# A two-layer hybrid attention trunk: TensorE's order written by hand as phases of the attention, instead of an order that a scheduler finds for whole blocks

## The chip, the cores and the metric

The kernel runs as one launch on one core of a Trainium2 chip. The metric is the device time of that launch in microseconds (us), the median over runs. The core has engines that run side by side and wait for one another by semaphores: TensorE (PE; its weight loads are listed as PEld), VectorE (DVE), ScalarE (ACT), GpSimd (POOL), and SyncE (SP), whose queue issues the transfers from DRAM.

## What is computed

One sequence of 256 tokens with 1024 features passes two layers. Eight heads of 64 columns ("MoBA") attend causally with a distance bias; eight more ("NSA", two groups of keys) sum three gated branches: compressed keys, selected blocks and a window. At 256 tokens every selection takes all that is causal, so the selected and the window branch are plain causal attentions over two sets of keys. The core of the reference:

```python
cs = silu(c)
for l in range(2):
    mod = cs @ w_ada[l] + b_ada[l]                       # 3072 columns
    shift, scale, gate = split(mod, 3)
    h = rmsnorm(x, g_pre[l]) * (1 + scale) + shift
    u = h @ w_in[l]                                      # 1024 x 3864
    qm, km, vm, zm, qn, kc, vc, ks, vs, kw, vw, gl, zn = split(u)
    o_m = softmax(causal(qm km' / 8 - slope * distance)) @ vm
    kc, vc = compress(kc), compress(vc)                  # 32-token windows, stride 16, two matmuls and a gelu
    o_n = g0 * attend(qn, kc, vc) + g1 * attend(qn, ks, vs) + g2 * attend(qn, kw, vw)
    y = concat(o_m * silu(zm), o_n * silu(zn))
    x = x + gate * rmsnorm(y @ w_out[l], g_post[l])
```

## The kernel before

**Projections.** Each projection is carried in two float32r parts of both operands: VectorE or ScalarE rounds a float32 tile to its high part, and VectorE subtracts to get the low part. `mm3` then issues three matmuls per row block of 128 features (low x high, high x low, high x high, L399 to L401). Weights come in units of 512 KB: a transfer into a `raw` tile (a pool of 8), the high part (`hi`, L364 on ScalarE or L366 on VectorE), the low part (`lo`, L372, VectorE). A chunk of 256 columns of `w_in` is two units and 48 matmuls. A chunk that is read with the weights stationary (`col_chunk`) does its columns in two halves of 24 matmuls.

**Modulation.** The sums of `silu(c) @ w_ada` are made in groups of 512 columns, four units of 512 KB each: either on VectorE, with 1 + 7 multiply-adds of 128x512 into `acc` (L231, L233) and four matmuls against ones (L240), or on TensorE with 32 small matmuls per group (L216). Then ScalarE copies the sums (`accr`, L245) and TensorE transposes them into columns (L252), so that VectorE can add the bias (L259).

**Attention.** An NSA block is two heads. Per head and token tile there are two score matmuls (L586, L587) into an `sc` bank of PSUM, and a softmax: VectorE adds the bias and takes the row's extreme (L545), ScalarE takes the exponential with its sum (L548), VectorE the reciprocal (L550) and the gate, and one of the two scales the row (L555, L557), all in an `S` tile (a pool of 3). Then three transposes on TensorE per branch (L565) and a copy to `PT` (L570, a pool of 3), and the value matmuls (L596, L602, L604) into the one `av` bank, of which head 0 writes the upper and head 1 the lower 64 partitions. The matmuls of the branches follow head after head. A MoBA block is the same with one branch (scores L615, L617, values L627, L630). `gate_out` (L637 to L641) multiplies by the gate path `z` and splits the result into `yH` and `yL`.

**The output.** `out_mm(0)` is 96 matmuls for the first 128 tokens, `out_mm(1)` 96 for the second. `post` squares the result on ScalarE (L309), takes the power -0.5 on POOL (L305), multiplies by the gate rows (L689) and updates `x` (L692). `hnorm` then squares `x` again, takes the power, scales (L322), transposes on TensorE (L336) and writes the next layer's `hH`, `hL` (L344 to L347).

**What sets the order.** Only the first layer's start (`first_layer_start`: the first modulation, the norm, and the first 2,000 or so columns) is issued in written order on all engines. What follows is a list of step names, `PLAN`. Each step emits whole blocks ("0nsa0", "0km0", "0out0"), and a tile scheduler moves the instructions of all engines, TensorE's too, as far as their dependencies and its own priorities let it; a choice of engine may be attached to a step (`:p` puts a modulation sum on TensorE, `:d` rounds the high parts on VectorE). The order about the layer boundary is "0out0 0post0 1h0 0out1 0post1 1V00 1h1 1V10".

## Time and profile before

| | us |
|---|---|
| median of three runs (lowest, highest) | 356.02 (354.57, 357.14) |
| span of the profiled execution, first to last instruction | 354.4 |
| TensorE busy | 341.4 |
| VectorE busy | 266.1 |
| ScalarE busy | 204.3 |
| POOL busy | 10.5 |

The profile is of one execution. Its span is 1.6 us under the median of the runs, within their spread; what lies before the first and after the last instruction is not in it, and no other time of this execution is listed. A busy TensorE is not the same as one at its best: matmuls overlap, and one that is listed with 0.28 us can follow the last by 0.12 us, so distances from start to start are what counts there. In the rows, "L399" is a line of the kernel, `pj<-hH,lo` says that a tile `pj` is written from `hH` and `lo`, and "xN" that N instructions are put together.

### The profile page before, as it was taken

The page shows a single profiled execution, that of the slowest core. Times are in us where ns is not written, and L with a number is a line of the kernel's source. Part 1 is how long each engine was busy: PE and PEld are TensorE (multiplying, and loading weights), DVE is VectorE, ACT ScalarE, POOL GpSimd, SP SyncE. Part 2 cuts the span into 40 slices and gives each one's busy share as a digit, 9 for nine tenths or more (in the row PEclk, how much of TensorE's full clock was granted, in tenths as well). Part 3 has the DMA queues.
Part 4 walks back from the last instruction along what each step waited for, and adds up shares of the span by engine and source line. Part 5 has one row for each costly group of instructions (what it writes and reads, how often), then busy time and mean ns, then how long its engine had stood idle before and what let it go on. Part 6 is the DMA issues. An engine that isn't in the chain of part 4 may idle for free.

```text
span 354.4 us, 7595 instructions
## 1 busy us (share of the span) xinstructions
PE 341.4 (96%) x2852; PEld 299.6 (85%) x2852; DVE 266.1 (75%) x727; ACT 204.3 (58%) x506; POOL 10.5 (3%) x23
## 2 busy tenths in 40 slices
PE   7999999999999999989999999999999999999993
PEld 7789889988887878767998999998878898677993
DVE  2648669999987898879898985999987646776132
ACT  4423407776989863757365455543889655668211
POOL 2000001100000000000011000000000000000000
PEclk9999999999999999999999999999999999999998
DMA  7999999939955566899755798489454330000111
GB/s 237 321 331 353 350 338 220 308 108 354 347 186 154 167 217 210 259 351 333 197 149 162 223 284 247 130 285 352 130 160 139 119 120 2 0 2 1 62 60 59
DMA packets 72060, 71.12 MB, mean 201 GB/s; under 512 B 11440, under 2 KB 61784, under 8 KB 72024
## 3 DMA queue, kind: packets, MB, share of 16 engines
q1 hardware_dynamic: 72024, 70.65, 64.1%
q8 instruction: 22, 0.36, 0.4%
q14 instruction: 14, 0.11, 0.1%
HBM read 69.58 MB, written 1.06 MB: 199 GB/s over the span
## 4 chain that ended last, share of the span: by engine, by line
PE 73%; DVE 13%; DMA 6%; issue 4%; ACT 2%; POOL 1%; SPq 1%; DVEq 0%; POOLq 0%; ACTq 0%
PE pj L399 13%; PE pj L400 13%; PE pj L401 13%; PE tr L565 5%; DVE lo L372 4%; PE av L602 3%; PE tr L216 3%; DMA yL<-in_w_ada_dram 2%; DMA raw<-in_w_out_dram 2%; PE av L627 2%; PE sc L586 2%; PE sc L617 2%; PE av L604 2%; PE pj L839 2%; PE av L596 2%
## 5 line engine op out<-in xcount | busy, mean ns | idle before, releaser
L372 DVE TENSOR_TENSOR lo<-raw,hi 128x1024 fp32r<-128x1024 f32 (+3 forms) x82 | 90.7, 1123 | 15.9 <-ACT hi L364 15.5
L399 PE MATMUL pj<-hH,lo 128*128 128x256 f32 x320 | 93.1, 291 | 0.0
L400 PE MATMUL pj<-hL,hi 128*128 128x256 f32 x320 | 92.5, 289 | 0.0
L401 PE MATMUL pj<-hH,hi 128*128 128x256 f32 x320 | 92.1, 288 | 0.0
L364 ACT CAST hi<-raw 128x1024 fp32r<-128x1024 f32 (+4 forms) x70 | 66.0, 966 | 22.7 <-PE pj L401 17.1
L399 PEld LDWEIGHTS pj<-hH,lo 128*128 128x128 f32 x320 | 61.0, 191 | 4.4 <-issue 3.4
L400 PEld LDWEIGHTS pj<-hL,hi 128*128 128x128 f32 x320 | 61.0, 191 | 2.2 <-issue 1.7
L401 PEld LDWEIGHTS pj<-hH,hi 128*128 128x128 f32 x320 | 61.0, 191 | 1.4 <-issue 1.1
L548 ACT ACTIVATE S<-S,mn 128x128 f32<-128x128 f32 (+1 forms) x96 | 42.7, 448 | 4.4 <-DVE mn L545 4.1
L233 DVE SCALAR_TENSOR_TENSOR acc<-raw,cs,acc 128x512 f32<-128x512 f32 x49 | 36.5, 747 | 1.6 <-DMA raw<-in_w_ada_dram 1.2
L545 DVE CUSTOM_DVE_ANT_0 S<-sc,bias 128x128 f32<-128x128 f32 (+1 forms) x96 | 31.6, 350 | 7.6 <-PE tr L565 3.1
L399 PE MATMUL pj<-hi,yL 128*128 128x256 f32 x112 | 31.9, 285 | 0.0
L401 PE MATMUL pj<-hi,yH 128*128 128x256 f32 x112 | 31.9, 286 | 0.0
L400 PE MATMUL pj<-lo,yH 128*128 128x256 f32 x112 | 31.8, 285 | 0.0
L565 PE MATMUL tr<-ident,S 128*128 128x128 f32 x144 | 29.6, 281 | 0.0
L570 ACT COPY PT<-tr 128x384 f32<-128x384 f32 x44 | 20.3, 478 | 10.0 <-PE tr L565 9.9
L565 PEld LDWEIGHTS tr<-ident,S 128*128 128x128 f32 x144 | 17.5, 140 | 6.7 <-issue 3.0
L555 ACT ACTIVATE S<-S,sm 128x256 f32<-128x256 f32 (+1 forms) x46 | 20.4, 483 | 2.9 <-DVE sm L550 1.4
L399 PEld LDWEIGHTS pj<-hi,yL 128*128 128x128 f32 x112 | 21.2, 189 | 0.9 <-issue 0.9
L401 PEld LDWEIGHTS pj<-hi,yH 128*128 128x128 f32 x112 | 21.1, 189 | 0.5 <-issue 0.5
L400 PEld LDWEIGHTS pj<-lo,yH 128*128 128x128 f32 x112 | 21.0, 188 | 0.3 <-issue 0.3
L548 ACT ACTIVATION_READ_ACCUMULATOR S<-S,mn 128x1 f32 x96 | 18.3, 190 | 0.0
(248 smaller groups left out, 650.1 us busy)
## 6 DMA issues: line engine op xcount, KB each, us to landing
raw<-in_w_in_dram SPq DMA_DIRECT2D x43, 512.0 KB, 4.5
raw<-in_w_ada_dram SPq DMA_DIRECT2D x32, 512.0 KB, 4.6
raw<-in_w_out_dram SPq DMA_DIRECT2D x16, 512.0 KB, 7.2
raw<-in_w_in_dram SPq DMA_DIRECT2D x9, 256.0 KB, 3.9
qs<-in_w_ada_dram SPq DMA_DIRECT2D x4, 512.0 KB, 7.2
yH<-in_w_ada_dram SPq DMA_DIRECT2D x4, 512.0 KB, 7.2
yL<-in_w_ada_dram SPq DMA_DIRECT2D x4, 512.0 KB
raw<-in_w_in_dram SPq DMA_DIRECT2D x9, 128.0 KB, 5.7
```

What stands on the lines that cost most here:

```text
L216: self.nc.tensor.matmul(pm[32 * r:32 * r + 32, :P], self.csz[:, k, :], raw[:, j, c * P:(c + 1) * P], start=first <= k < first + turns, sto ...
L233: nc.vector.scalar_tensor_tensor(out=out, in0=raw[:, j], scalar=self.cs[:, k:k + 1], in1=out, op0=OP.mult, op1=OP.add)
L364: self.nc.scalar.copy(hi[:, :nk * n], raw[:, :nk * n])
L372: self.nc.vector.tensor_sub(lo[:, :nk * n], raw[:, :nk * n], hi[:, :nk * n].bitcast(F32))
L399: nc.tensor.matmul(out, aL, bH, start=first, stop=False)
L400: nc.tensor.matmul(out, aH, bL, start=False, stop=False)
L401: nc.tensor.matmul(out, aH, bH, start=False, stop=last)
L545: nc.vector.tensor_tensor_reduce(out=s[:, a:b], in0=sc[:, a:b], in1=self.bias[:, h, S - (b - a):S], scale=-1.0, scalar=3.0e38, op0=OP.add, ...
L548: nc.scalar.activation(s[:, a:b], s[:, a:b], AF.Exp, bias=mn[:, i:i + 1], scale=-1.0, accum_out=sm[:, i:i + 1])
L555: nc.scalar.activation(s[:, a:b], s[:, a:b], AF.Copy, scale=sm[:, i:i + 1])
L565: nc.tensor.transpose(pt[:, i * P:(i + 1) * P], blk, self.ident)
L570: nc.scalar.copy(ps, pt[:, :3 * P])
```

## The change

After the first layer's start, TensorE's instructions are issued in the written order; the other engines are still ordered by the scheduler. The steps are cut smaller. `nSbj` is the scores and softmax of NSA block b, head j; `nTbj` its six transposes in a row; `nVb` the block's values, with the two heads alternating. `mSb`, `mTb`, `mVb` are the same of a MoBA block, both heads together. `c0` to `c4` are the five pieces of the compressed branch. Names with a point are pieces of projections of 24 matmuls ("zn1.0"; the out pieces have 12 or 24). `g0`, `g1`, `x1` to `x4` are the ends of modulation groups; their weights are fetched and summed on VectorE (`ada_start`) from the place of the group before. Weights of a projection are fetched and split four pieces ahead of the first use (`AHEAD`). The plan:

```python
PLANS = ["""
c0 nS00 zn1.0 nS01 c1 g0 zn1.1 nT00 c2 nS10 vm.0 nT01 c3 vm.1 nS11 km0.0 c4 nT10 nS20 km0.1 nV0 g1
nT11 qm0.0 nS21 nV1 G qm0.1 nT20 nS30 zm0.0 nT21 nS31 zm0.1 nV2 x0 x1 km1.0 nT30 mS0 km1.1 nT31 x2
qm1.0 nV3 mT0 mS1 qm1.1 mV0 x3 zm1.0 mT1 mS2 zm1.1 mV1 x4 out0.0 out0.1 mT2 mS3 out1.0 mV2 out1.1
mT3 out1.2 mV3 out0.2 out0.3 post0
out1.3 out1.4 out1.5 post1
""", """
h0 A.0 V0.0 V1.0 h1 A.1 V0.1 V1.1 K.0 K.1 Q0.0 Q0.1 nS00 C.0 nS01 C.1 nT00 Q1.0 c0 nT01 Q1.1 c1
nS10 zn0.0 c2 nS11 zn0.1 c3 qm0.0 nT10 c4 qm0.1 nV0 nS20 km0.0 nT11 nS21 km0.1 nV1 g0 nT20 zn1.0
...
```

The core of the diff:

```diff
-        pm = self.tl(self.ps, [P, 512], "tr", bufs=2)
-        if on_pe:
-            for i, raw in enumerate(units):
-                self.ada_on_pe(pm, spec, i, raw)
-        else:
-            self.ada_sum(pm, self.ada_on_dve(spec, units))
-        self.ada_cols(spec, self.ada_rows(pm))
+    def ada_end(self, spec):
+        acc = self.acc.pop(spec[0])
+        pc = self.tl(self.ps, [P, 512], "tr", bufs=2)
+        for j in range(4):
+            self.nc.tensor.matmul(pc[:, j:j + 1], acc[:, j * P:(j + 1) * P], self.ones[:, 0:1],
+                                  start=True, stop=True)
+        self.ada_mod(spec, pc[:, :4])
...
-        for i in range(2):
-            for j in range(2):
-                o = av[j * HD:(j + 1) * HD, :]
-                vc = slice(i * P + g * HD, i * P + (g + 1) * HD)
-                nc.tensor.matmul(o[:, :S], self.vsw[:, 0, vc], pts[j][i][:, :S],
-                                 start=False, stop=False)
-                nc.tensor.matmul(o[:, P:S], self.vsw[:, 1, vc], pts[j][i][:, S:],
-                                 start=False, stop=(i == 1))
+        for kt in range(2):
+            for i in range(2):
+                vc = slice(i * P + g * HD, i * P + (g + 1) * HD)
+                for j in range(2):
+                    if kt == 0:
+                        nc.tensor.matmul(o[j][:, :S], self.vsw[:, 0, vc], pts[j][i][:, :S],
+                                         start=False, stop=False)
+                    else:
+                        nc.tensor.matmul(o[j][:, P:S], self.vsw[:, 1, vc], pts[j][i][:, S:],
+                                         start=False, stop=(i == 1))
...
+            if c == "out0":
+                c = "out0" if int(t.split(".")[1]) < (2, 3)[int(t[3])] else "out1"
+            if (l, c) not in seen:
+                seen.add((l, c))
+                loads.setdefault(pieces[max(0, at - AHEAD)], []).append((l, c))
+        adas = [i for i, (_, t) in enumerate(steps) if t[0] in "gx" and t != "x0"]
+        for at, i in enumerate(adas):
+            before = adas[at - 1] + 1 if at else 0
+            loads.setdefault(before, []).append(steps[i])
...
-            self.rp = self.pool("raw", bufs=8)
+            self.rp = self.pool("raw", bufs=5)
...
-            self.wp = self.pool("work", bufs=3)
-            self.pp = self.pool("probT", bufs=3)
+            self.wp = self.pool("work", bufs=6)
+            self.pp = self.pool("probT", bufs=6)
...
             with self.tc.manual_schedule():
                 started = self.first_layer_start()
-            self.first_layer_rest(*started)
-            for token in PLAN:
-                self.step(token)
+            with self.tc.manual_schedule(engines={mybir.EngineType.PE}):
+                self.first_layer_rest(*started)
+                self.after_start()
```

`work` holds the `S` tiles of the softmax. The choices of engine by step are gone: transposed probabilities are always copied by ScalarE, and the high parts of weights are rounded on VectorE in two chunks only (`1V0`, `1V1`). In layer 0 all modulation groups are now summed on VectorE.

The first place at which the order changes is TensorE's, right after the first layer's start. `pj_936` and `pj_1071` are the chunk "zn1", L469 and now L482 the first matmul of the compressed branch (with `cmpR` and its weights `raw`), L605 and L606 NSA scores. TensorE before:

```order
L437 MATMUL tr_895<-ident,pe_892 128x32
L399 MATMUL pj_936<-hH_167,lo_928 128x256
L400 MATMUL pj_936<-hL_168,hi_926 128x256
L401 MATMUL pj_936<-hH_167,hi_926 128x256
...
L469 MATMUL sc_995<-cmpR_897,raw_987 64x33
L469 MATMUL sc_995<-cmpR_897,raw_989 64x33
```

And TensorE with the change:

```order
L450 MATMUL tr_897<-ident,pe_894 128x32
L482 MATMUL sc_951<-cmpR_899,raw_943 64x33
L482 MATMUL sc_951<-cmpR_899,raw_945 64x33
...
L605 MATMUL sc_1001<-wide_885,qs_135_911 128x256
L606 MATMUL sc_1001<-wide_884,qs_135_911 128x256
...
L418 MATMUL pj_1071<-hH_167,hi_1031 128x256
```

The 48 matmuls of "zn1", which stood ahead of the compressed branch, are now behind it and behind the first scores.

The transfers moved with it. In SyncE's queue of before the weights of "zn1" (`raw_924`, `raw_930`) go out during the first layer's start; now they stand behind a modulation group and the compressed branch's weights, which take six places of a pool of five. SyncE with the change, where `raw_1029` and `raw_1035` are "zn1":

```order
L212 DMA raw_932<-in_w_ada_dram 128x2x512
L473 DMA raw_943<-in_w_ck_dram 128x16x64
L473 DMA raw_945<-in_w_cv_dram 128x16x64
L478 DMA w_145_947<-in_w_cv_dram 64x64
...
L447 DMA pe_3111<-in_pe_v_dram 16x128
L373 DMA raw_1029<-in_w_in_dram 128x4x256
L373 DMA raw_1035<-in_w_in_dram 128x4x256
L373 DMA raw_1041<-in_w_in_dram 128x3x280
```

The program makes `raw_1029` and `raw_1035` wait for TensorE's last reads of `raw_943` and `raw_945`, which are the L482 matmuls above.

The second place is VectorE's order at the layer boundary. `x_97` and `x_99` are the two token tiles of the residual, `pj_2494` and `sc_2376`/`sc_2401` pieces of `out1`, `wide_2462` and `wide_2601` the scaled `x` that `h0` transposes. VectorE before:

```order
L692 SCALAR_TENSOR_TENSOR x_97<-wide_2444,rstd_2452,x_97 128x512
...
L303 SCALAR_TENSOR_TENSOR rstd_2466<-ssq_2463 128x1
L372 TENSOR_TENSOR lo_2617<-raw_2613,hi_2615 128x1024
L322 TENSOR_SCALAR wide_2462<-x_97,rstd_2466 128x512 x2
...
L689 TENSOR_TENSOR wide_2593<-pj_2494,modG_1868 128x512
```

VectorE with the change:

```order
L730 SCALAR_TENSOR_TENSOR x_97<-wide_2492,rstd_2500,x_97 128x512 x2
...
L727 TENSOR_TENSOR wide_2578<-sc_2401,modG_1598 128x256
L730 SCALAR_TENSOR_TENSOR x_99<-wide_2578,rstd_2591,x_99 128x512 x2
L320 SCALAR_TENSOR_TENSOR rstd_2605<-ssq_2602 128x1
L389 TENSOR_TENSOR lo_2700<-raw_2695,hi_2698 128x1024
L339 TENSOR_SCALAR wide_2601<-x_97,rstd_2605 128x512 x2
```

`h0`'s norm (`rstd_2466`, now `rstd_2605`) stood ahead of `post1`; now the whole of `post1`, up to the update of `x_99`, stands ahead of it.

The third is TensorE's order at the same boundary (L336, now L353, are `h0`'s transposes). Before, the transposes lie among the matmuls of `out1`:

```order
L336 MATMUL tr_2472<-ident,wide_2462 128x128 x4
L336 MATMUL tr_2483<-ident,wide_2462 128x128 x4
...
L401 MATMUL pj_2495<-hi_1734,yH_1148 128x256
...
L401 MATMUL sc_2496<-hi_2314,yH_1148 128x256
...
L401 MATMUL pj_2625<-hi_2615,hH_2458 128x256
```

With the change they follow the last of `out1`, and the next layer's chunk "A" follows them at once:

```order
L418 MATMUL sc_2376<-hi_2269,yH_999 128x256
...
L418 MATMUL sc_2401<-hi_2275,yH_999 128x256
L353 MATMUL tr_2611<-ident,wide_2601 128x128 x4
L353 MATMUL tr_2622<-ident,wide_2601 128x128 x4
...
L418 MATMUL pj_2633<-qm_2450,hH_2597 128x280
```

Between `out0`'s last matmul and `h0`'s transposes there are now 48 matmuls of `out1` (`out1.3` to `out1.5`); the other 48 come before `out0.2`.

## Rows read from the trace of the kernel before

**Rows 1.** The page's chain that ended last: shares of the span by engine.

```profile
PE 73%; DVE 13%; DMA 6%; issue 4%; ACT 2%; POOL 1%; SPq 1%; DVEq 0%; POOLq 0%; ACTq 0%
```

**Rows 2.** Waits of TensorE, longest sums: us in total, times, longest.

```profile
PE tr L252 <- ACT accr L245: 2.0, 3, 1.2
PE tr L336 <- DVE wide L322: 1.2, 2, 0.7
PE pj L400 <- DVE lo L372: 0.9, 1, 0.9
```

**Rows 3.** Stretches of the span: length, busy us by engine, granted clock, DMA share, GB/s.

```profile
75.50:174.70 99.20, 97.86 (x791) 81.27 (x792) 86.12 (x274) 69.52 (x191) 0.00 (x0) 1.00 0.79 253
240.00:348.50 108.50, 108.34 (x815) 91.31 (x813) 69.03 (x241) 64.89 (x183) 0.55 (x1) 1.00 0.28 91
348.50:351.00 2.50, 0.03 (x1) 0.00 (x0) 1.48 (x4) 0.47 (x2) 0.55 (x1) 1.00 0.00 0
351.00:354.40 3.40, 0.00 (x0) 0.00 (x0) 0.43 (x1) 0.00 (x0) 0.00 (x0) 0.51 0.40 154
```

**Rows 4.** VectorE's groups by line and shape: count, busy us, mean ns.

```profile
L372 DVE TENSOR_TENSOR lo<-raw,hi 128x1024 fp32r<-128x1024 f32 x67 | 81.0, 1218 | 15.9 <-ACT hi L364 15.5
L233 DVE SCALAR_TENSOR_TENSOR acc<-raw,cs,acc 128x512 f32<-128x512 f32 x49 | 36.5, 747 | 1.6 <-DMA raw<-in_w_ada_dram 1.2
```

**Rows 5.** Timeline of TensorE at an NSA block: start us, us, instructions.

```profile
101.68 0.66 PE L602 MATMUL av<-PT,vsw 128*64 128x256 f32 x4
102.16 0.40 PE L604 MATMUL av<-PT,vsw 128*64 128x128 f32 x4
102.38 0.59 PE L602 MATMUL av<-PT,vsw 128*64 128x256 f32 x2
102.81 0.38 PE L604 MATMUL av<-PT,vsw 128*64 128x128 f32 x2
103.12 0.44 PE L565 MATMUL tr<-ident,S 128*128 128x128 f32 x2
...
104.47 0.28 PE L401 MATMUL pj<-hH,hi 128*128 128x256 f32 x1
104.68 0.65 PE L596 MATMUL av<-pct,vx 128*64 128x256 f32 x4
105.26 0.39 PE L399 MATMUL pj<-hH,lo 128*128 128x256 f32 x1
105.48 0.28 PE L400 MATMUL pj<-hL,hi 128*128 128x256 f32 x1
```

**Rows 6.** Timeline after the first layer's start, TensorE and VectorE.

```profile
66.25 0.25 PE L437 MATMUL tr<-ident,pe 32*128 32x32 f32 x1
...
70.88 0.19 DVE L450 COPY cmpR<-tr 128x16 f32<-128x16 f32 x1
...
72.37 2.06 PE L469 MATMUL sc<-cmpR,raw 128*64 128x33 f32 x64
...
73.94 0.69 DVE L753 SCALAR_TENSOR_TENSOR z<-z,tr 128x512 f32<-128x512 f32 x1
```

**Rows 7.** The page's DMA issues of 512 KB: KB, median us to landing.

```profile
raw<-in_w_in_dram SPq DMA_DIRECT2D x43, 512.0 KB, 4.5
```

**Rows 8.** Timeline of the layer boundary: VectorE, POOL, TensorE.

```profile
174.68 0.69 DVE L689 TENSOR_TENSOR wide<-pj,modG 128x512 f32<-128x512 f32 x1 [0.22 <-ACT S L309]
...
180.24 1.47 POOL L305 TENSOR_TENSOR rstd<-rstd,half 128x1 f32<-128x1 f32 x1 [2.95 <-DVE rstd L303]
181.74 0.88 DVE L322 TENSOR_SCALAR wide<-x,rstd 128x512 f32<-128x512 f32 x2 [0.45 <-POOL rstd L305]
182.37 1.07 PE L336 MATMUL tr<-ident,wide 128*128 128x128 f32 x8 [0.55 <-DVE wide L322]
```

**Rows 9.** The first stretches of TensorE, its warming matmuls of 128 columns (L283) alone.

```profile
2.50:6.30 3.80, 3.73 (x17) 3.74 (x18) 1.00 0.93 338
6.30:7.30 1.00, 1.00 (x11) 1.00 (x9) 1.00 0.98 280
```

More of the change, by code (lines that the diff above doesn't have):

```diff
@@ new lines, in piece @@
+    def piece(self, l, c, i):
+        if c[:3] == "out":
+            return self.out_piece(int(c[3]), i)
+        n = int(c[-1]) if c[-1].isdigit() else 0
+        w = self.w[c]
+        if c == "vm":
+            self.tok_mm(i, w, self.ev_v(self.VM0, 512))
+        elif c == "A":
+            self.tok_mm(i, w, self.ev_a)
+        elif c[0] == "V":
+            if self.first("vm", l):
+                self.vm = self.tl(self.mp, [P, NT, 512], "vm")
+            self.tok_mm(i, w, self.ev_v(256 * n, 256 * n + 256))
+        elif c[:2] in ("zn", "zm"):
+            side = c[1] == "n"
+            if self.first(c[:2], l):
+                self.z[side] = self.tl(self.mp, [P, 4, S], f"z{side:d}")
+            self.col_piece(w, i, self.ev_z(side, n))
+        elif c[:2] in ("qm", "km"):
@@ new lines, in step @@
+            {"nS": self.nsa_scores, "nT": self.nsa_turn, "nV": self.nsa_values,
+             "mS": self.moba_scores, "mT": self.moba_turn, "mV": self.moba_values}[kind](*n)
+        elif kind == "g":
+            self.ada_end(self.spec(token))
+        elif kind == "x" and n[0] == 0:
+            self.mod_rows()
+        elif kind == "x":
+            self.ada_end(self.spec(token))
+        elif kind == "G":
+            self.G = self.gate_rows()
+        elif kind == "post":
+            self.post(l, n[0], self.pos(n[0]), self.G)
+        elif kind == "h":
+            if n[0] == 0:
+                self.start_layer()
+            self.hnorm(n[0])
@@ new lines, in spec, with plan @@
+    def spec(self, token):
+        i = int(token[1:])
+        return [(2, 4 * i, 4)] if token[0] == "g" else [((i - 1) // 2, 4 * ((i - 1) % 2), 4)]
+    def plan(self):
+        steps = [(l, t) for l, p in enumerate(PLANS) for t in p.split()]
+        pieces = [i for i, (_, t) in enumerate(steps) if "." in t]
+        loads = {}
+        seen = set()
+        for at, i in enumerate(pieces):
+            l, t = steps[i]
+            c = t.split(".")[0]
+            if c == "out1":
+                c = "out0"
+            if c == "out0":
[7 more added lines that the diff above has]
+            loads.setdefault(before, []).append(steps[i])
+        rows = [i for i, (_, t) in enumerate(steps) if t == "x0"][0]
+        loads.setdefault(rows - 20, []).append((0, "rows"))
+        return steps, loads
@@ new lines, in after_start @@
+    def after_start(self):
+        steps, loads = self.plan()
+        for i, (l, t) in enumerate(steps):
+            for ll, c in loads.get(i, ()):
+                if c == "rows":
+                    self.load_mod_rows(1)
+                elif c[0] in "gx":
+                    self.ada_start(ll + (c[0] == "x"), self.spec(c))
+                else:
+                    self.load_chunk(ll, c)
+            if "." in t:
+                c, p = t.split(".")
+                self.piece(l, c, int(p))
+            else:
+                self.step(l, t)
```

304 lines of the change are left out of this document (137 added, 167 removed).

## The prediction

> **What bounds the kernel now.** I read the chain first, then TensorE's waits, then stretches of the span, then single places. The chain is 73% TensorE and 13% VectorE [rows 1]. TensorE's listed waits come to about 6 us in all, and the largest sum is 2.0 us [rows 2], so over the whole span it is the bound, and what can be won on it must come from the length of its own work. The stretches tell more [rows 3]. Between 75.5 and 174.7 us, the attention and the projections of layer 0, TensorE is busy 97.9 of 99.2 us, but VectorE is busy 86.1 as well: there it is a second bound close behind. Between 240 and 348.5, the same part of layer 1, TensorE is busy 108.3 of 108.5 us and VectorE only 69.0. So a gain on TensorE counts in full in layer 1, and in layer 0 only as far as VectorE lets it. The reader is to keep these two halves apart.
>
> **The change part by part.**
>
> *TensorE's own work.* A break between float32r projections and a float32 piece costs time on both sides. At 104.47 the last projection matmul is followed after 0.21 us, and at 105.26 the first one after a break is followed by the next after 0.22 us [rows 5]; in a run of one kind 256 columns take 0.12 (four L602 in 0.48, same rows). So a break costs about 0.09 + 0.10 = 0.19 us. Counted in the two orders from the end of the first layer's start, TensorE leaves the projections 120 times before and 45 times with the change: 75 x 0.19 = 14.3 us. Alternating heads: four matmuls of 256 and four of 128 columns with alternating heads take 0.70 us (101.68 to 102.38), two and two of one head 0.74 (102.38 to 103.12) [rows 5]. Two and two alternated would be 0.35, so a group of four gains 0.39. The values of both layers are 192 such passes, 48 groups, at most 18.7 us; in the block shown only a third was not alternated already, so 6; the MoBA scores, which now alternate too, I put at 2. Together with some sums and transposes of the modulation that go (at most 2 us, within the range), I take 24 us off TensorE, 13 in layer 0 and 11 in layer 1; the bounds are 14 (breaks alone) and 35.
>
> *VectorE's work in layer 0.* Between the evacuation of the first gate path (73.94 [rows 6]) and `post0`'s first multiplication (174.68 [rows 8]) VectorE's two orders differ so: 13 more multiply-adds of 128x512, one more first product, 5 more low parts of 1024 columns, two of 840 and one of 560, one rounding to high parts; the rest nearly cancels. They come from the modulation groups that were summed on TensorE or later, and from low parts that are now made before the boundary. At 0.747 and 1.218 us [rows 4]: 13 x 0.75 = 9.8, 5 x 1.22 = 6.1, by width 2 x 1.0 and 0.7, and at most 0.75 and 1.2 for the other two: 20.5. Neighbours overlap a little, so I use 18, with 16 and 20.5 as bounds. The stretch was busy 86.1 us plus the 1.6 before its start, 87.7 of 100.7. With 18 more it is 105.7: the multiplication can't come before 73.9 + 105.7 = 179.6, even if VectorE never waits. It waited 13.0 us before. With twice the softmax buffers and weights fetched four pieces ahead I take a third of that, 4 us: 183.6, or +8.9; bounds +3 (16, no wait) and +20 (18, the old wait). So the 13 us that TensorE saves here are not seen at all.
>
> *The start of that stretch.* TensorE comes free at 66.25; VectorE ends `cmpR` at 70.88 + 0.19 = 71.07; the compressed branch's matmuls take 2.1 us [rows 6]. Before, the 48 matmuls of "zn1" covered the wait. Now nothing does, and "zn1" has no weights until those matmuls release its two buffers: issued at 73.2, 4.5 us to landing [rows 7], a rounding and a low part of at most 1.2 each: 80.1. TensorE idles 4.8 + 6.2 = 11.0 us less the 0.7 of the first scores, about 10. That costs nothing beyond the above: TensorE would have 174.7 - 13 + 10 = 171.7, plus 5.8 for the 48 matmuls of `out1` that now go ahead of `out0`'s end, 177.5, which is still under VectorE's 179.6. It only takes away the slack. If the transfer lands in 2 us, the wait is 7.5, and nothing changes.
>
> *The layer boundary.* P is `post0`'s first multiplication. Before, `h0`'s transposes start 7.7 us after it (182.37 [rows 8]), and TensorE has 96 matmuls of `out1`, 11.5 us, to cover that; the two waits for the scaled `x` are 1.2 us together [rows 2]. Now 48 are left, 5.8 us, and end at about P + 7 (`out0` ends 1 us after P). On VectorE `h0`'s norm is queued behind all of `post1`: a square (0.6), a power on POOL (up to 1.47 [rows 8]; I take 1.0), two updates of `x` at 0.75, then the norm's own square, power (1.47) and the first scaling (0.5): P + 12.5. TensorE idles 5.5. "A" then follows the transposes at once, and must wait for all of `hH` and `hL` of that token tile: I estimate 4 us (twelve pieces of 0.3 to 0.7 us on two engines, with a POOL power of the second tile queued in front of `hL`), and 2 more at "A.1" behind `h1`. In all 11.5 us idle in the place of 1.2, less the 5.8 that were done earlier: +4.5. Bounds 0 (VectorE, freer by now, makes the pieces at once) and +8.
>
> *Layer 1.* TensorE saves 11. New waits: the first scores stand directly behind the queries' chunk (2 us); `c4` has one piece of 24 matmuls and six transposes as cover, 3.5 us, for a chain on VectorE in which six multiply-adds and one low part are mixed, 6 x 0.75 + 1.2 + 2.5 = 8.2: 4.7 us; transposes that wait for one of two banks, 2. About 9, bounds 2 and 12. Net -2. VectorE has room [rows 3]. The tail after TensorE's end, 348.5 to 354.4, is unchanged.
>
> **The sum.** +8.9 +4.5 -2 = +11.4 us on the profiled span of 354.4: 365.8. The median of the runs stands 1.6 above it, so 367; I say 366, since the waits in layer 0 are the softest term.
>
> **The rivals.**
>
> *The waits are hidden and layer 1 wins (faster).* If VectorE never idles in layer 0 (+3), the boundary is covered by VectorE's freed time (0 to +1) and layer 1 keeps all but 2 of its 11 us (-9), the sum is -5: 351. It decides from the point where `post0` comes before 179 and layer 1's new waits stay under 4 us. For it: VectorE's 69.0 of 108.5 in layer 1 [rows 3]. Against: the order at the boundary is fixed and has no other work in it. More than this can't come, since 24 us would need VectorE to do 18 us more in no time. Chance 0.16.
>
> *It cancels.* VectorE at +5, the boundary +4, layer 1 -8: within 1% of before, 357 (about 1%, 3.6 us, is what a measurement of this kernel can tell from no change). Chance 0.17.
>
> *TensorE's clock falls in the new waits.* [...] Up to now the longest of the waits shown is 1.2 us [rows 2]; now there would be three of 4 to 6 us or more. At the beginning 17 matmuls of 128 columns take 3.8 us and the next 11 only 1.0 [rows 9], 0.22 against 0.09 each: 17 x 0.13 = 2.2 us lost per fall. The one at the start is hidden by VectorE; the two at the boundary are not: +4.4, or 371. [...] Chance 0.25.
>
> *The change does not do what it says.* If the 0.19 us of a break is not the switch itself but a wait for data that comes anyway, TensorE saves only the alternation, some 8 us, 4 in each layer; layer 0 stays at VectorE's time, and layer 1 gives +5 in the place of -2: 373. Against it: the same 0.2 us stands at every switch in the rows, with no wait listed. Chance 0.07.
>
> **How the numbers follow.** The forecast as worked out has 0.35, the clock 0.25 and the last rival 0.07: slower by over 1% 0.67. Within 1% 0.17, faster by over 1% 0.16. The softest costs give the ends: VectorE's idle time (+3 to +20), the boundary (0 to +8) and layer 1 (-9 to +1) don't all fall to one side, so I take 352 (the faster rival's end) to 380 (clock, and half of the upper bound of VectorE's wait). The likeliest case alone is 360 to 373.
>
> **What would show it.** In the profile of the changed kernel: TensorE busy some 320 us; a wait of 4 us or more of TensorE for `cmpR` at 66, and one for the first `lo` near 73 to 80; VectorE busy over 95% between 74 and `post0`; `post0`'s first multiplication at 180 to 188; a wait of about 5 us of L353 on the scaled `x` and one of 3 to 5 of "A" on `hL`; waits of about 5 us at `c4` in layer 1; granted clock under 1.00 in slices at the boundary if the clock rival holds. It is wrong if `post0` comes before 179, if VectorE idles over 10% in layer 0 while TensorE waits for something else (another queue, a transfer), or if L353 waits under 2 us.

## The result, and the profile after

| | before | with the change |
|---|---|---|
| median of four runs (us) | 356.31 | 388.7 (387.22 to 390.23) |
| ratio, 95% interval | | 1.092 (1.0875 to 1.0973) |
| span of the profiled execution | 354.4 | 385.5 |
| mean granted clock of TensorE | 0.995 | 0.929 |

The change makes the kernel slower by 32 us, 9%. The forecast was 366 us with a range of 352 to 380: the direction was right, the size was not. One run of e13 below lay 1.8% above the fastest of its kernel and is left out of its median and interval. The page of the changed kernel, its busy times, the 40 slices of TensorE and of the granted clock (full marks are 9), and the chain by engine, which answers to [rows 1]:

```profile
PE 336.9 (87%) x2788; PEld 309.1 (80%) x2788; DVE 269.7 (70%) x723; ACT 210.5 (55%) x510; POOL 8.9 (2%) x23
...
PE   7999999557989998999992869978949999999993
...
PEclk9999999656899999899995689999988999999998
...
PE 62%; DVE 13%; DMA 11%; ACT 8%; issue 4%; SPq 1%; POOL 1%; DVEq 0%; POOLq 0%; ACTq 0%
```

TensorE is busy 337 us, hardly less than before, and yet its busy time is worth less: in three places the busy digits fall, and in the same places the digits of the clock fall, to 5 and 6 in the first two and to 8 in the third. One more 8 of the clock, in the 17th slice, has no such place. Before, the clock's digits were all 9 but for the last. TensorE's waits, which answer to [rows 2] (us in total, times, longest):

```profile
PE pj L416 <- DVE hL L364: 7.4, 2, 4.3
PE tr L353 <- DVE wide L339: 5.8, 1, 5.8
PE tr L557 <- DVE S L550: 5.8, 1, 5.8
PE sc L482 <- DVE cmpR L463: 3.6, 1, 3.6
PE pj L416 <- DVE lo L389: 3.5, 1, 3.5
PE tr L292 <- DVE kbd L510: 2.9, 1, 2.9
PE sc L605 <- DVE qs L775: 2.7, 1, 2.7
PE tr L591 <- ACT pct L560: 1.5, 1, 1.5
PE sc L605 <- DVE hid L488: 1.4, 1, 1.4
```

Every row names VectorE or a copy behind it. The first two are the layer boundary (h0's and h1's `hL`, and h0's scaled `x`), the third is `c4` in layer 1, the fourth to sixth and the last are the start of layer 0, the seventh the first scores of layer 1, the eighth (at 114.28 us) still the compressed branch of layer 0. The stretches, in the columns of [rows 3] (length, busy us of PE, PEld, DVE, ACT and POOL, granted clock, DMA share, GB/s), cut at the start of layer 0, at 100 us, at `post0`'s first multiplication and at "A.1" behind `h1`:

```profile
67.90:75.10 7.20, 3.41 (x58) 3.23 (x58) 6.95 (x13) 3.24 (x7) 0.00 (x0) 0.72 0.31 60
75.10:100.00 24.90, 16.74 (x88) 14.97 (x85) 22.89 (x63) 14.40 (x33) 0.00 (x0) 0.60 0.87 271
100.00:194.20 94.20, 91.52 (x754) 83.07 (x755) 84.13 (x238) 63.13 (x165) 0.00 (x0) 0.98 0.82 255
194.20:229.00 34.80, 21.67 (x155) 20.91 (x154) 18.11 (x36) 14.11 (x35) 3.05 (x4) 0.79 0.27 76
229.00:378.80 149.80, 138.93 (x1180) 129.47 (x1180) 91.76 (x265) 88.85 (x218) 0.55 (x1) 0.97 0.38 113
```

TensorE's idle time in these rows is 3.8 + 8.2 + 2.7 + 13.1 + 10.9 = 38.7 us. The clock of a row is a mean over idle time too, so what the lower clock cost is read from the stretches in which the granted clock was 0.50, the lower of the two levels in this trace:

```profile
71.09:88.16 17.07, 11.36 (x93) 10.23 (x94) 16.21 (x43) 9.19 (x19) 0.00 (x0) 0.50 0.65 196
91.57:98.40 6.83, 6.20 (x29) 6.23 (x30) 5.58 (x14) 2.27 (x5) 0.00 (x0) 0.50 0.82 267
153.01:156.42 3.41, 3.41 (x18) 3.41 (x17) 3.34 (x6) 0.00 (x0) 0.00 (x0) 0.50 0.94 310
204.21:217.86 13.65, 5.99 (x25) 5.65 (x26) 7.98 (x16) 4.09 (x11) 1.94 (x2) 0.50 0.41 115
228.10:231.52 3.42, 2.90 (x12) 2.93 (x13) 1.06 (x2) 0.62 (x2) 0.00 (x0) 0.50 0.02 5
286.13:292.96 6.83, 3.13 (x15) 3.17 (x16) 4.21 (x10) 0.37 (x1) 0.00 (x0) 0.50 0.92 268
```

TensorE is busy 33.0 us in them. Half of that, 16.5 us, is lost, an estimate by the two granted clocks, 0.50 and 1.00: 8.8 at the start of layer 0, 1.7 at 153 us, 4.4 in the two stretches about the boundary, 1.6 at `c4`. Without it TensorE's busy time would be 320 us, 21 less than before. In the first 32 us alone it lost 12.0 us idle and 8.8 to the lower clock.

The place of the first L353, the boundary (start us, us, in brackets the idle time before):

```profile
207.54 1.94 PE L353 MATMUL tr<-ident,wide 128*128 128x128 f32 x8 [5.77 <-DVE wide L339]
...
213.81 0.57 PE L416 MATMUL pj<-qm,hL 128*128 128x280 f32 x1 [4.33 <-DVE hL L364]
...
224.55 1.04 PE L353 MATMUL tr<-ident,wide 128*128 128x128 f32 x8
228.62 0.57 PE L416 MATMUL pj<-qm,hL 128*128 128x280 f32 x1 [3.03 <-DVE hL L364]
```

The eight transposes behind the 5.8 us wait take 1.94 us at a granted clock of 0.50, the eight of `h1`, which follow on matmuls, 1.04 at 1.00; in [rows 8] they took 1.07. `post0`'s first multiplication, at 174.68 before [rows 8], is at 194.05: 19.4 us later. Of these, 5.8 are the 48 matmuls of `out1` that were moved ahead of it. So the 31.1 us of the two spans are about 13.6 in layer 0, 14.9 at the boundary and 2.7 in layer 1. For the boundary: "A.1" starts 34.6 us after that multiplication; before, the same work was done 25.4 us after it, when this matmul began; the 5.8 us of `out1`, done earlier now, come on top of the difference.

```profile
200.11 0.28 PE L399 MATMUL pj<-hi,hL 128*128 128x256 f32 x1
```

### The profile page after: what moved, and what is told of

It reads as the page before. It is cut to its first block, busy times and chain, and to the rows that moved or that the text cites. A ratio compares the mean times of both kernels' runs of the same rounds, so it can differ in the third digit from the quotient of the medians.

```text
span 385.5 us, 7446 instructions
## 1 busy us (share of the span) xinstructions
PE 336.9 (87%) x2788; PEld 309.1 (80%) x2788; DVE 269.7 (70%) x723; ACT 210.5 (55%) x510; POOL 8.9 (2%) x23
## 4 chain that ended last, share of the span: by engine, by line
PE 62%; DVE 13%; DMA 11%; ACT 8%; issue 4%; SPq 1%; POOL 1%; DVEq 0%; POOLq 0%; ACTq 0%
PE pj L416 13%; PE pj L417 12%; PE pj L418 12%; DMA yL<-in_w_ada_dram 4%; DVE lo L389 4%; PE tr L591 3%; DMA raw<-in_w_in_dram 3%; ACT hi L381 3%; PE tr L292 2%; PE av L630 2%; DMA km<-in_w_ada_dram 2%; PE sc L416 2%; PE sc L482 2%; DMA qs<-in_w_ada_dram 2%; ACT S L574 1%
## 5 line engine op out<-in xcount | busy, mean ns | idle before, releaser
L381 ACT CAST hi<-raw 128x1024 fp32r<-128x1024 f32 (+4 forms) x76 | 72.5, 969 | 18.8 <-PE pj L418 9.3
L416 PEld LDWEIGHTS pj<-hH,lo 128*128 128x128 f32 x320 | 64.5, 202 | 7.8 <-DVE lo L389 4.2
L417 PEld LDWEIGHTS pj<-hL,hi 128*128 128x128 f32 x320 | 64.4, 201 | 0.6
L418 PEld LDWEIGHTS pj<-hH,hi 128*128 128x128 f32 x320 | 64.4, 201 | 0.0
L245 DVE SCALAR_TENSOR_TENSOR acc<-raw,cs,acc 128x512 f32<-128x512 f32 x56 | 41.7, 745 | 1.2 <-DMA raw<-in_w_ada_dram 0.7
L416 PE MATMUL pj<-hi,yL 128*128 128x256 f32 x96 | 27.3, 284 | 0.0
L418 PE MATMUL pj<-hi,yH 128*128 128x256 f32 x96 | 26.8, 279 | 0.0
L417 PE MATMUL pj<-lo,yH 128*128 128x256 f32 x96 | 26.8, 279 | 0.0
L581 ACT ACTIVATE S<-S,sm 128x256 f32<-128x256 f32 x48 | 22.3, 501 | 3.7 <-DVE sm L578 3.5
L591 PE MATMUL tr<-ident,S 128*128 128x128 f32 x144 | 20.6, 276 | 2.1 <-ACT pct L560 1.5
L591 PEld LDWEIGHTS tr<-ident,S 128*128 128x128 f32 x144 | 16.1, 141 | 3.3 <-ACT pct L560 1.7
```

The source lines that it names most:

```text
L245: nc.vector.scalar_tensor_tensor(out=out, in0=raw[:, j], scalar=self.cs[:, k:k + 1], in1=out, op0=OP.mult, op1=OP.add)
L381: self.nc.scalar.copy(hi[:, :nk * n], raw[:, :nk * n])
L416: nc.tensor.matmul(out, aL, bH, start=first, stop=False)
L417: nc.tensor.matmul(out, aH, bL, start=False, stop=False)
L418: nc.tensor.matmul(out, aH, bH, start=False, stop=last)
L581: nc.scalar.activation(s[:, a:b], s[:, a:b], AF.Copy, scale=sm[:, i:i + 1])
```

## The experiments

All are versions of the changed kernel, timed beside the kernel before (355.2 to 356.0 us in these comparisons). The first four groups, and e8, keep TensorE's written order. Of the plan's long lines the edits show only the part that differs, joined where the plan breaks the line. Gains are differences of medians from the changed kernel's 388.7; by the ratios they are up to 1.1 us smaller. Differences under 4 us (e1, e4, e6, e13, e14, e18) lie within the two intervals or at their edge. `post0` stands for the start of its first multiplication, in one profile each; in the changed kernel, e4 and e7, whose layer 0 is the same, it is at 194.0, 197.2 and 194.4, so 3 us there say nothing.

**The three places, one at a time.** e1 puts the first chunk back to the front, with its weights:

```diff
-c0 nS00 zn1.0 nS01 c1 g0 zn1.1 nT00 c2 nS10 vm.0 nT01 c3 vm.1 nS11 km0.0 c4 nT10 nS20 km0.1 nV0 g1
+zn1.0 zn1.1 c0 nS00 vm.0 nS01 c1 vm.1 nT00 c2 nS10 km0.0 nT01 c3 km0.1 nS11 qm0.0 c4 nT10 g0 nS20
...
-            before = adas[at - 1] + 1 if at else 0
+            before = adas[at - 1] + 1 if at else pieces[2]
```

> The weights of zn1 and of the compressed branch are fetched first, zn1's 48 matmuls stand again between the first layer's start and the compressed branch, and every later piece of layer 0 moves up by two places. Theory A (the waits of TensorE at the start, 12 us, and the low clock after them, about 6 us, are what set layer 0's end): post0's first multiplication comes 10 to 14 us earlier than the 194 of the changed kernel, limited by VectorE's 107 us of work (74 + 107 = 181), granted clock 1.00 between 66 and 100 us, and the time falls from 389 to 375 to 380. Theory B (VectorE's own work is the bound in layer 0 and hides the start, as the prediction had it): post0 moves by 0 to 3 us, the time stays at 386 or above.

Measured: 387.4 us, ratio 1.092 (1.088 to 1.096); `post0` at 192.8. Neither the wait for `cmpR` nor that for "zn1" is left, but others have come:

```profile
PE tr L596 <- DVE kbd L515: 5.8, 1, 5.8
...
PE sc L610 <- DVE hid L493: 3.5, 1, 3.5
```

The time is in theory B's range, but the waits aren't hidden as B says: they have moved to the next steps of the compressed branch and are as long as those that went (9.3 us for 7.1).

e2 puts the boundary back:

```diff
-mV1 x4 out0.0 out0.1 mT2 mS3 out1.0 mV2 out1.1 mT3 out1.2 mV3 out0.2 out0.3 post0 out1.3 out1.4 out1.5 post1
-h0 A.0 V0.0 V1.0 h1 A.1 V0.1
+mV1 x4 mT2 mS3 out0.0 mV2 out0.1 mT3 mV3 out0.2 out0.3 post0 out1.0 out1.1 out1.2 h0 out1.3 out1.4 out1.5 post1
+V0.0 V1.0 h1 A.0 A.1 V0.1
```

> Only the layer boundary is put back: all 96 matmuls of out1 behind out0's end, h0's norm and transposes ahead of post1 and among them, then V0.0, V1.0, h1 and only then A.0. Theory A (the order there costs 13 us of idle TensorE and 4 at half rate): waits of TensorE at L353 and on hL fall from 13.2 us to under 4, some 2 to 3 us are given back in front of out0.2, where out1 was the cover of the last softmax; time 389 to 379 to 382. Theory B (VectorE's chain of post0, post1 and the norms is the bound and the idle time only moves): gain under 3 us.

Measured: 382.6, ratio 1.077 (1.073 to 1.082): 6 us back, just short of theory A. L353 and `hL` are waited for 4.6 us in the place of 13.2. Part of that is lost again in front of `post0`, which is still at 195.0 though 5.8 us of `out1` no longer precede it: between 170 and 195 us TensorE, which has lost the cover of the last softmax, is idle for 3.9 us at a mean clock of 0.86.

e4 moves `c4` in layer 1:

```diff
-qm0.0 nT10 c4 qm0.1 nV0 nS20 km0.0 nT11
+qm0.0 nT10 qm0.1 km0.0 c4 nV0 nS20 nT11
```

> In layer 1 the last piece of the compressed branch (c4) is moved behind two more pieces of projections (qm0.1, km0.0), 5.8 us of cover more. Theory A (a wait and the low clock after it): the 5.8 us wait of L557 on VectorE goes to under 1.5, the clock stays at 1.00 around 290, gain 6 to 8 us: 381 to 383. Theory B (the wait moves to the next piece, since VectorE's chain with six multiply-adds in it is late for everything): gain under 3 us.

Measured: 384.8, ratio 1.084 (1.079 to 1.090): 4 us back, between the two theories. The wait of L557 is 1.3 in the place of 5.8, and no stretch of lower clock is left at that place. In this profile `post0` came 3 us later than in the changed kernel, although only layer 1 was edited; from there to the end it takes 4.1 us less.

**The clock.** e3 and e7 move nothing and fill TensorE's waits with matmuls that nobody reads. The edit of e7 (Wn is n of them; e3 had 24 ahead of zn1.0 and about twice these numbers):

```diff
+        elif kind == "W":
+            self.warm(int(i))
...
-h0 A.0 V0.0 V1.0 h1 A.1 V0.1
+W24 h0 W18 A.0 V0.0 V1.0 h1 W13 A.1 V0.1
...
-nT10 c4
+nT10 W25 c4
```

> Nothing is moved; matmuls of 128 columns that nobody reads fill TensorE's waits (24 ahead of zn1.0, 50 ahead of h0's transposes, 36 ahead of A.0, 26 ahead of A.1, 50 ahead of c4's transposes in layer 1). Theory A1 (part of the loss is the half-rate stretch after each wait): granted clock 1.00 between 200 and 235 us and around 290, 24 us less at the low level, 5 to 8 us faster than the changed kernel: 381 to 384. Theory A2 (only the waits count, the half-rate work lies beside VectorE's): within 2 us of 389.

Measured: 397.9, ratio 1.121 (1.117 to 1.125), slower: the size was wrong. Each dummy matmul is listed as two of 0.11 us, so they ran on beyond the waits, up to 5 us past them. At the start "zn1" was then done at a granted clock of 1.00, its matmuls 0.12 us apart, but c1 waited for `kbd` (3.7 us) as before, and `post0`, at 192.2, is not clearly earlier.

> Nothing is moved; the dummy matmuls in TensorE's waits are halved against the run e3, where each was listed as two of 0.11 us and they ran past the waits (now 24 ahead of h0's transposes, 18 ahead of A.0, 13 ahead of A.1, 25 ahead of c4's, none at the start; 5.4, 4.0, 2.9 and 5.6 us). Theory A1 (the half-rate stretch after a wait is part of the loss): granted clock 1.00 from 200 to 235 and about 290, time 5 to 7 us under the changed kernel: 382 to 384. Theory A2 (it lies beside other work): 387 to 390.

Measured: 382.6, ratio 1.077 (1.071 to 1.082): 6 us back, as A1 expected, without one step being moved. Stretches of e7, then the same of the changed kernel:

```profile
194.00:235.00 41.00, 39.95 (x336) 39.41 (x335) 22.16 (x40) 19.03 (x44) 3.05 (x4) 1.00 0.27 74
280.00:296.00 16.00, 15.82 (x138) 14.84 (x137) 12.27 (x34) 7.71 (x20) 0.00 (x0) 1.00 0.83 250
```

```profile
194.00:235.00 41.00, 27.87 (x195) 27.11 (x194) 19.20 (x38) 15.81 (x40) 3.05 (x4) 0.79 0.24 66
280.00:296.00 16.00, 10.24 (x79) 9.47 (x79) 11.56 (x25) 8.47 (x19) 0.00 (x0) 0.79 0.70 213
```

The granted clock is 1.00 in the place of 0.79 in both. That the lower clock after a wait costs time of its own is shown here, for the boundary and `c4`: the 6.0 us that were read above for these places come back (5.6 by the ratios). The start was not filled.

**VectorE's load and its queue, order still written.** e6 takes the eight multiply-adds of layer 1's first modulation group out of the end of layer 0; e17 takes layer 0's first group out of its beginning; e14 asks for the compressed branch later; e13 loads later.

```diff
+            if steps[i] == (1, "g0"):
+                before = [k for k, s in enumerate(steps) if s == (1, "Q0.1")][0]
             loads.setdefault(before, []).append(steps[i])
```

> Only the eight multiply-adds of layer 1's first modulation group are taken out of the end of layer 0 (their weights are fetched and summed from layer 1's chunk Q0 on). Theory V (VectorE's work sets layer 0's end): post0's first multiplication moves from 194 to 188 to 190, time 383 to 385. Theory P (TensorE's waits and half-rate stretches at the start set it, VectorE has slack by then): post0 within 1.5 us, time within 2 us of 389.

Measured: 391.6, ratio 1.100 (1.096 to 1.105). `post0` is at 194.1 as in the changed kernel, and before it TensorE is busy without a gap and VectorE is not:

```profile
180.00:194.20 14.20, 14.20 (x122) 12.80 (x121) 10.37 (x25) 7.24 (x20) 0.00 (x0) 1.00 0.68 186
```

So VectorE's total does not set the end of layer 0: it was busy 101.8 us between 75 us and there, 5 less, and the end did not move. The 3 us lost are in layer 1, where the first scores now wait 4.4 us for `qs` in the place of 2.7, and where the clock is lower for longer (0.81 from 229 to 262 us in the place of 0.96).

```diff
-c0 nS00 zn1.0 nS01 c1 g0 zn1.1 nT00 c2 nS10 vm.0 nT01 c3 vm.1 nS11 km0.0 c4 nT10 nS20 km0.1 nV0 g1
+c0 nS00 zn1.0 nS01 zn1.1 nT00 nS10 c1 vm.0 nT01 c2 g0 vm.1 nS11 c3 km0.0 nT10 km0.1 c4 nS20 nV0 g1
```

> In layer 0 the pieces c1 to c4 stand one piece of projections later, behind zn1.1 and the next scores; loads as in the changed kernel. VectorE's work is the same. Theory Q (a written order that asks for a late step too early): the wait on kbd goes, TensorE does zn1.1 in its place, post0 3 to 5 us earlier (189 to 191), time 383 to 386. Theory V (VectorE's total sets post0): post0 within 1.5 us of 194, time within 2 us of 389.

Measured: 391.3, ratio 1.100 (1.095 to 1.105); `post0` at 196.9. The wait on `kbd` is gone, and in its place stands a second one for L557, of 2.0 us (the sum was 5.8):

```profile
PE tr L557 <- DVE S L550: 7.7, 2, 5.8
```

Theory Q falls in the form that it had: later is not better. The time is just outside theory V's range too.

```diff
-AHEAD = 4
+AHEAD = 2
```

> Only AHEAD goes from 4 to 2 pieces. In the changed kernel VectorE makes six low parts (of zn1, vm and km0, 6.5 us) before it copies kbd, for which TensorE's c1 waits in written order until 91.9. With 2 ahead the two low parts of km0 come after it. Theory Q (what VectorE has queued ahead of the branch's small steps sets the start, not its total): the wait on kbd falls from 2.9 to under 1, post0 comes 2 to 4 us earlier, time 384 to 387, if later weights are still in time. If two pieces are too few for a transfer, a rounding and a low part (3.7 + 1.0 + 1.2 against 5.8 us), new waits on lo of 1 us each at most of the 28 chunks and 392 or more.

Measured: 386.3, ratio 1.085 (1.079 to 1.090). With runs between 384.2 and 388.0 this is no clear gain, and no theory is told apart by it.

```diff
-c1 g0 zn1.1 nT00
+c1 zn1.1 nT00
...
-nV0 g1 nT11 qm0.0 nS21 nV1 G qm0.1 nT20
+nV0 g0 nT11 qm0.0 nS21 nV1 g1 qm0.1 nT20 G
...
-            before = adas[at - 1] + 1 if at else 0
+            before = adas[at - 1] + 1 if at else steps.index((0, "c3"))
```

> TensorE's order as in the changed kernel, but the first modulation group of layer 0 (g0: four transfers and eight operations of VectorE, 6 us) starts at c3 in the place of the very beginning, and g0, g1 and G end later. Theory V1 (in the first 30 us VectorE's own queue is the bound, and the written order makes TensorE wait for it): zn1.0 starts at 77 to 79 in the place of 82.7, the wait on kbd ends at 86 to 88 in the place of 91.9, post0 4 to 7 us earlier, time 381 to 385. Theory M (waits only move, as in e1 and e14): post0 within 2 us of 194, time 387 or more.

Measured: 395.6, ratio 1.112 (1.105 to 1.119), 7 us slower than the changed kernel; `post0` at 200.0. The first step is as V1 expected ("zn1" starts at 78.1), and then new waits follow, at sums (L292), at transposes (L591, 2.6 us) and at the compressed branch (L482, L524):

```profile
PE tr L292 <- DVE sm L576: 3.8, 2, 2.1
...
PE sc L482 <- ACT qs L773: 3.0, 1, 3.0
PE tr L524 <- ACT PT L593: 2.8, 1, 2.8
```

Theory V1 falls. Of theory M the time holds, but `post0` did not stay, it came 6 us later: here the waits have not only moved but grown. I read this as an order that was written for one timing of VectorE and gets worse when that timing changes; one case does not show it.

**Heads.** e18 lets the values go head after head again:

```diff
-        for kt in range(2):
-            for i in range(2):
-                vc = slice(i * P + g * HD, i * P + (g + 1) * HD)
-                for j in range(2):
+        for i in range(2):
+            vc = slice(i * P + g * HD, i * P + (g + 1) * HD)
+            for j in range(2):
+                for kt in range(2):
```

> TensorE's order as in the changed kernel, only the NSA values go head after head again (128 passes in 32 pairs of one head). By the price of the forecast (0.74 us for two and two of one head against 0.35 alternated) 32 groups of four cost 0.39 each: 12 us more work on TensorE; where TensorE is the bound (layer 1, and layer 0 from 100 us on) most of it shows: 397 to 402. If the pairs lie in time that TensorE has anyway, or the 0.39 is an effect of something else: 389 to 392.

Measured: 389.0, ratio 1.094 (1.090 to 1.098): the same as the changed kernel. A block's values in e18, then in the changed kernel:

```profile
139.61 0.65 PE L623 MATMUL av<-pct,cmpR 128*64 128x256 f32 x4
140.09 0.65 PE L630 MATMUL av<-PT,vsw 128*64 128x256 f32 x4
140.53 0.44 PE L633 MATMUL av<-PT,vsw 128*64 128x128 f32 x4
140.74 0.65 PE L630 MATMUL av<-PT,vsw 128*64 128x256 f32 x4
141.18 0.44 PE L633 MATMUL av<-PT,vsw 128*64 128x128 f32 x4
141.54 0.25 PE L193 MATMUL tr<-ident,modrows 40*128 40x40 f32 x1
```

```profile
138.96 0.65 PE L623 MATMUL av<-pct,cmpR 128*64 128x256 f32 x4
139.44 1.03 PE L630 MATMUL av<-PT,vsw 128*64 128x256 f32 x8
140.31 0.61 PE L633 MATMUL av<-PT,vsw 128*64 128x128 f32 x8
140.84 0.25 PE L193 MATMUL tr<-ident,modrows 40*128 40x40 f32 x1
```

1.93 us against 1.88. What the forecast read in [rows 5] as the price of single heads is not that. The MoBA blocks, and the compressed branch's values, still alternate in e18; they were not tested.

**The order free.** e5 undoes one line of the change:

```diff
-            with self.tc.manual_schedule(engines={mybir.EngineType.PE}):
-                self.first_layer_rest(*started)
-                self.after_start()
+            self.first_layer_rest(*started)
+            self.after_start()
```

> One line is undone: TensorE's order is left to the scheduler again; steps, buffers (raw 5, S 6, PT 6), loads four pieces ahead, alternating heads and the modulation sums on VectorE stay as in the changed kernel. Theory S (the strictness of TensorE's order costs the waits: what stands behind a late operand may not pass it): TensorE's listed waits fall from 46 us to under 15, time 389 to 350 to 365. Theory V (VectorE's added work and the smaller raw pool are the bound in layer 0, whoever orders TensorE): time 370 to 385, VectorE still over 88% busy between 75 us and post0.

Measured: 367.5, ratio 1.034 (1.030 to 1.038): 21 of the 32 us are back, with the steps, buffers, loads and modulation as they are. The time lies between the two theories. TensorE's listed waits are 27 us in the place of 43, where theory S had under 15; VectorE is 87% busy before `post0`. The longest waits:

```profile
PE tr L353 <- DVE wide L339: 11.8, 2, 8.8
PE sc L482 <- DVE cmpR L463: 3.5, 1, 3.5
PE sc L605 <- DVE sm L578: 1.9, 1, 1.9
```

The waits on `hL` and at L557 are gone, those on `qs` and `pct` under 1 us; at the boundary 11.8 us are left of 13.2, now all at L353. `post0` is still at 194.1, but some 45 more matmuls of `out1` now lie ahead of it, about 5 us of work: a part of what is won lies ahead of `post0`, the rest behind it. The breaks between projections and float32 pieces, 45 in the written order, are 73 now (120 before the change).

e9 frees the order and puts the boundary back as in e2; e11 also puts zn1 first as in e1; e10 is e8 (e1, e4 and e6 and a boundary like e2's, in written order) with the order free; e12 is e9 with 6 raw and 4 S buffers.

> The edits of e1 (zn1 and the branch's weights first), e2 (out1 and h0 at the boundary, here with 36 matmuls ahead of h0), e4 (c4 later) and e6 (layer 1's first group later) together. Theory: with the waits at the three places closed the gains add, about 6 at the boundary, 6 at c4, 5 from VectorE and 2 at the start: 368 to 373. If the waits only move on to the next step that needs VectorE: 376 to 384. Neither gives a time under the kernel before.

Measured: 371.2, ratio 1.044 (1.040 to 1.049), as the first theory expected: in written order the four edits together give 17.5 us, while alone they gave 1.3, 6.1 and 3.9 and (e6) cost 2.9.

> TensorE's order free as in e5, and the boundary's steps as in e2 (all of out1 behind out0's end, h0 among it and ahead of post1). Theory A (in e5 12.3 us of waits are left, all at the two L353, since post1 is still written ahead of h0, and some 4 us of half rate behind them): waits at L353 under 3 us, time 367.5 to 354 to 358. Theory B (what is left of e5's 12 us lies at the start, 66 to 95 us, and the boundary's waits only move): 363 or more.

Measured: 362.0, ratio 1.018 (1.015 to 1.022), between the two theories: 5.5 us under e5. L353 is waited for 1.2 us, but `hL` for 5.2 in its place.

> All edits of e8 (zn1 first, boundary, c4 later, layer 1's first group later) with TensorE's order free. If the places were each a price of their own, this and e9 are the same but for the start: 348 to 353, under the kernel before (355.5), since the 20 us that the phases and alternating heads take off TensorE remain where the scheduler keeps the phases together. If the scheduler breaks the phases up again (more than 80 breaks between projections and float32 pieces), the gain is gone: 354 to 360.

Measured: 360.6, ratio 1.015 (1.011 to 1.018). The breaks are 91: the second case, and a little slower than that.

> As e9 with zn1 and the branch's weights first as in e1, and nothing else of e8. Against e9 it tells the start apart: in e9 TensorE waits 3.5 us for cmpR and works at the lower clock from 71 to about 82. Theory A (the start is a loss of its own, 5 us of waits and 4 of half rate): 4 to 8 us under e9. Theory B (VectorE is full from 66 to 100 us, so what TensorE gets earlier it waits for later, as in e1): within 2 us of e9.

Measured: 365.7, ratio 1.028 (1.025 to 1.031), slower than e9: neither theory. Work at the lower clock and waits at the start are gone, breaks rise from 78 to 93, and the boundary waits 5.1 us for L353 again.

> As e9 with one more raw buffer (6) and two fewer S buffers (4). If the smaller raw pool keeps weights late (transfers that wait for a free buffer, ScalarE's rounding waiting for them), 2 to 5 us under e9. If the six S buffers are what lets the softmax run ahead, as many us over it. Within 1.5 us: neither matters once the order is free.

Measured: 360.2, ratio 1.013 (1.010 to 1.016): 1.8 us under e9, between the cases. Which of the two edits gives it is not told apart.

e15 adds to e12 the later `c4` and layer 1's later group, e16 also AHEAD = 2.

> TensorE free, the boundary of e2, c4 later, layer 1's first group later, raw 6 and S 4: e12 with two of e10's edits. If their gains add to e12's 360.2 (e10 had 5 us less than e11 with these two): 355 to 358, no better than the kernel before. If they were e10's start alone: 360 or above.

Measured: 358.5, ratio 1.007 (1.005 to 1.009): 1.7 us under e12, nearer to the first case, though short of the 5 us that the two gave between e11 and e10.

> As e15 with weights two pieces ahead in the place of four. If early low parts ahead of more urgent work on VectorE are what is left of the loss: 1 to 4 us under e15, and the first version under the kernel before (355.5). If the scheduler needs the early weights to have work to choose from: 2 us or more over e15.

Measured: 356.8 (ten runs), ratio 1.0023 (0.9998 to 1.0048): no different from the kernel before, and not under it. No version that ran beats the kernel before.

## Why the prediction was right or wrong

The forecast added up three stretches. "Idle" and "lower clock" are what TensorE lost in them with the change (us; the lower clock is the estimate above):

| stretch | forecast | measured | idle | lower clock |
|---|---|---|---|---|
| layer 0, up to `post0`'s first multiplication | +8.9 | +19.4 | 14.6 | 10.5 |
| from there to "A.1" | +4.5 | +9.1 | 13.1 | 3.0 |
| from "A.1" to the end | -2 | +2.7 | 10.9 | 3.0 |

**The bound.** Right that a gain of TensorE is not seen in layer 0, wrong about why. The prediction had VectorE's total as the bound. Its size was right (107.0 us busy between 75.1 and 194.2 us, 105.7 forecast), but that is 90% of the stretch, where over 95% had been the sign, and e6 took 5 us of it away ahead of `post0` and `post0` stayed. The measured +19.4 is no support for VectorE's upper bound of +20 either: by its own numbers ("18, the old wait") that bound is +18.

**The step that failed is "The start of that stretch", with the clock's term in it.** It held a wait of 10 us on TensorE (11 by its own numbers: the 0.7 of the first scores is taken off twice) and said "That costs nothing beyond the above", with TensorE's path at 177.5, under VectorE's 179.6. In the profile TensorE's path is the longer one. In the same terms it is 174.7, plus 1.6 for a later end of the first layer's start, less 11.0 saved, plus 12.5 more idle than before, plus 10.5 at the lower clock, plus the 5.8 of `out1`: 194.1, where 183.6 was forecast. The saving in this sum is worked back from the other terms (see below). The two waits that were worked out were near (`cmpR` 3.6 for 4.8, and "zn1" starts at 82.7 for 80.1); `hid`, `kbd` and `pct` added 5.8 behind them. The largest term that the forecast's path lacked, the 10.5 of the lower clock, stood at nothing: "The one at the start is hidden by VectorE". From 100 us on TensorE, not VectorE, is full (91.5 of 94.2 us), so what it lost before is not caught up.

**TensorE's saving.** Forecast 24 us, 13 and 11. Worked back from the stretches it is about 22: 11 in layer 0 (14.6 idle + 10.5 at the lower clock + 1.6, less 2.1 idle before, against 13.6 late) and 11 in layer 1 (10.9 + 3.0, less 0.2, against 2.7 late). The busy times, with the lower clock taken off, differ by 21. The sum was right, one of its parts was not: alternating the heads of the selected and window values gives nothing (e18). What remains is the fewer breaks (14 forecast) and what else the phases save. That each break costs 0.19 us was not tested alone.

**The boundary.** The waits were forecast at 11.5 us and are 13.1 (5.8 for 5.5, 4.3 for 4, 3.0 for 2). The lower clock behind them, which I had put into a rival at 4.4, costs 4.4, of which 1.4 lie behind the start of "A.1". Both are shown: e2, which takes away most of the waits, and e7, which keeps the clock up there and at `c4`, give back 6 us each.

**Layer 1.** Forecast -2, measured +2.7: `c4` waits 5.8 us (4.7 forecast, its low part and multiply-adds as counted), the first scores 2.7 (2), and the lower clock adds 3.0, which the sum did not have.

**The clock as a rival.** I gave it 0.25 and 4.4 us. It should have stood in the main case: it costs 16.5 us, and the forecast missed by 20 on the span. At the boundary and at `c4` e7 shows that cost; at the start of layer 0 no run shows by itself what it would give back. Five of the six falls lie in waits of 2.9 to 5.8 us; the one at 153.01 us has only 1.15 us of idle time close ahead of it, and the 2.7 us wait for `qs`, at 253.20, has no fall (1.00 from 232 to 286 us). What sets off a fall is not shown. The 2.2 us per fall in the rival was my estimate from the first matmuls; no run shows it, and [rows 9] list a granted clock of 1.00 in both stretches. In the changed kernel the six falls cost 1.4 to 5.7 us each, by the estimate above.

**What stays open.** Why layer 0 is late as a whole isn't settled by a single edit. Moving the start (e1, e14), filling a wait in it (e3) and lightening VectorE at either end (e6, e17) each leave `post0` at 192.2 to 200. With TensorE's order free, the start of e11 has neither waits nor lower clock (33.3 of 34 us busy at 1.00), and its time is not better for it. `post0` is earliest, at 178.2, with the order free, a larger raw pool and later loads (e16); 4 us of that are some 34 matmuls of `out1` that no longer lie ahead of it. I read this as many small dependencies on VectorE, of which a fixed order always meets the next one, but only the sum is shown. Of the 32 us, 21 are TensorE's written order (e5); the other 11 lie in what e9, e12, e15 and e16 take back step by step, and the single shares of buffers and loads are not told apart.

## What to carry to other kernels

In this kernel TensorE was busy 96% of the span with a second engine nearly full beside it. What looked like disorder in its order (120 breaks) also filled its waits; the tidy written order has 45 breaks and waits of 3 to 6 us. When a wait of some microseconds on TensorE is forecast, price the matmuls behind it at the lower clock with it (here the granted clock was 0.50 for 3.4 to 17.1 us at five waits of 2.9 to 5.8 us), and do not call it hidden before adding up that engine's own path with this price in it. When an edit removes a wait and the time stays, look which step waits now before calling the wait free.

## What the runs showed of the hardware

The granted clock fell in waits in the middle of the changed kernel, to 0.50 in five of them: matmuls of 280 columns behind the 4.3 us wait at 213.81 stand 0.23 us apart at first and 0.13 later, at a granted clock of 0.50 and then 1.00:

```profile
215.12 0.44 PE L418 MATMUL pj<-qm,hH 128*128 128x280 f32 x1
215.35 0.44 PE L416 MATMUL pj<-qm,hL 128*128 128x280 f32 x1
...
218.16 0.29 PE L417 MATMUL pj<-lo,hH 128*128 128x280 f32 x1
218.29 0.29 PE L418 MATMUL pj<-hi,hH 128*128 128x280 f32 x1
```

Matmuls that nobody reads kept it at 1.00 through the waits at the boundary and at `c4`, and that alone was worth 6 us (e7). One fall has no long wait ahead of it: at 153.01 us the granted clock goes to 0.50 for 3.4 us, and matmuls of 256 columns stand 0.21 us apart in the place of 0.12. Ahead of it TensorE did six transposes, sat idle for 1.15 us, made the sums of a modulation's end and began a projection.

The float32 matmuls of one column were no cheap thing here: the four of a modulation's end are listed as eight and take 1.05 us at a granted clock of 1.00, 0.13 each, as much as a transpose of 128 columns (the eight at 224.55 take 1.04):

```profile
151.44 1.05 PE L292 MATMUL tr<-ones,acc 128*128 128x1 f32 x8 [1.15 <-ACT PT L593]
```
